# Transposed activations with four row tiles side by side, and weight slots that begin at multiples of 128 bytes

## The chip, the cores and the metric

The kernel runs on one core of a Trainium2 chip. The metric is the device time of one execution in microseconds; the time before is 1054.98 us, the median of 3 runs (1054.74 to 1055.16). Lower is better.

## What is computed

One layer of a hybrid decoder, for 1024 rows (positions) of 1024 features, all in float32:

```python
h = rms_norm(x, mix_norm)
z = h @ w_in                       # 1024 x 2320: gq, gk, gv, gr, glr, sq, sk, sv
o_gla = gla_chunked(gq, gk, gv, log_a)            # 4 heads, chunks of 64
o_gla = rms_norm(o_gla, gla_norm) * silu(gr)
o_swa = swa_sink_attention(sq, sk, sv, sinks)     # 8 heads, window 128
x = x + concat([o_gla, o_swa]) @ w_out
h2 = rms_norm(x, ffn_norm)
u = causal_dwconv(h2 @ w_up, conv_w, conv_b)      # 1024 x 5632, three taps
a, b = split(u, 2)
return x + (silu(a) * b) @ w_down                 # 2816 x 1024
```

## The kernel before

Every large product is made in float32r with each operand split into a high part and a low part (`split`, `tr_hi`, `tr_lo`: the high part is a copy rounded to float32r, the low part the difference). A product of two such operands is three passes of matmuls, `PASSES = ((0, 0), (0, 1), (1, 0))`, which sum in one PSUM bank. The 1024 rows are 8 row tiles `t` of 128, the 1024 features 8 tiles `k` of 128.

**The activations.** `big` holds the transposed activations of the stage that runs: features on the 128 partitions, and in each partition for each row tile `t`, feature tile `k` and part `r` (0 high, 1 low) 128 float32 values of the rows. It is filled three times: by the first norm (`norm1_tr`, `norm1_lo`), by the mixer's output (`gate_tr`), and by the second norm (`norm2_tr`, `norm2_sums`). A write covers four feature tiles `k` of one row tile and one part, that is four pieces of 128 values. `ex` holds three more such operands for the feed-forward part: sums and differences of quarters of the transposed activations, made in `norm2_sums`.

**The dense stages.** In `dense` (L317; the first three q tiles go through `unit_q_part`, L707) the weights that TensorE loads are 128 x 128 tiles of `big`, and the moving operand is a 128 x 512 tile of split weights. One row tile takes 8 feature tiles x 3 passes = 24 matmuls of 512 columns; for k and v of the window attention (tiles dk) the columns are 272. The names in the profile: dq, dk, dv, dg, dr for the parts of `w_in`, do for `w_out`.

**The feed-forward part.** `w_up` is taken in 22 chunks of 128 columns for a and 128 for b. Each chunk is a 2 x 2 block product by Strassen's scheme, seven products P1 to P7 (`product`, L834) of 4 feature tiles x 3 passes = 12 matmuls. Here the roles are turned round: the loaded weights are 128 x 128 tiles of the chunk's split operand (A11, A12, A22, S1 to S4), and the moving operand is 512 rows, four row tiles at once, of `big` (B11, B21, B22, T1) or `ex` (T2, T3, T4), given by `b_operand`. `w_down` goes by pairs of chunks with seven products too (`down_pair`, L1015, six matmuls at a time, both operands in slots): from chunk 2 on, one such piece of six follows each up product of twelve. The last two chunks go through `last_row` (L1044), where both operands are in slots and nothing comes from `big`.

**The order.** All work is entered in a list of events with times (`at`, `at_us`), which are sorted once, and a dependency-tracking layer places it on the engines' queues; no queue order depends on addresses.

**The places in the memory.** Nearly all split weights and the split gate live in nine slots of 4096 bytes a partition (`slot_tile`, pool `wa`: high part 2048 bytes, low part 2048 bytes), which lie at the upper end of the memory. The pool on the right side is filled from the upper end down. The memory that tiles can have ends at byte 229344 of a partition, which is 96 past a multiple of 128, so that before, with the slots uppermost, each slot begins 96 bytes past a multiple of 128 (192480, 196576, ...). `big` begins at 1152 and `ex` at 112448, both multiples of 64. The first two up operands of chunk 1 (`A11w_1`, `A12w_1`) are not in a slot but in the pool of the second norm, at multiples of 64; the weights of dk lie, but for the last feature tile, in a tile `kw` that begins at a multiple of 64 and has rows of 1088 bytes, a multiple of 64.

`mhalf` is a constant tile, -0.5, the exponent of the power that GpSimd takes in `rms_scale` and `norm1_stat`; it is at most 8 columns wide in use.

Of the kernel before, what the change touches and what calls it, by code (L numbers as in the profile page):

```python
# [9 lines left out]
F32 = mybir.dt.float32  # L10
F32R = mybir.dt.float32r
# [6 lines left out]
P = 128  # L18
T = 1024
D = 1024  # L20
NT = T // P
KD = D // P
# [12 lines left out]
def hymba_layer_kernel(ctx, tc, x, mix_norm, w_in, w_alpha2, b_alpha, gla_norm,  # L35
# [3 lines left out]
    act, dve, pool, pe, sp = nc.scalar, nc.vector, nc.gpsimd, nc.tensor, nc.sync  # L39
# [10 lines left out]
    base = ctx.enter_context(tc.tile_pool(name="base", bufs=1))  # L50
# [4 lines left out]
    def bank(name):  # L55
        ps["n"] += 1
        if "f" in ps:
            return ps["f"][2 + ps["n"] % 2]

        for start, which in (("n2pt_6", "b"), ("do1_7", "a"), ("n2pt_3", "a")):  # L60
            if name.startswith(start):
                return ps[which].tile([P, 512], F32, tag="b", name=name)
        return ps["ab"[ps["n"] % 2]].tile([P, 512], F32, tag="b", name=name)

    big = base.tile([P, NT, KD, 2, P], F32R, name="big")

    RAW_BUFS, K4, K2, N_WARM = 3, 6, 5, 5

    def raw_tile(name):
        return base.tile([P, 1024], F32, tag="raw", name=name, bufs=RAW_BUFS)  # L70

    w_keep = ctx.enter_context(tc.tile_pool(name="wa", bufs=1, side="right"))
    w_late = {}
    swp = ExitStack()
    idp = swp.enter_context(tc.tile_pool(name="idp", bufs=1, side="right"))
# [14 lines left out]
    def split(src, hi, lo, eng=None, hi_eng=None):  # L90
        if hi_eng is None:
            act.copy(hi, src)
        else:
            hi_eng.tensor_copy(hi, src)
        (eng or pool).tensor_sub(lo, src, hi.bitcast(F32))  # L95
# [19 lines left out]
    upper = gl.tile([P, P], F32, name="upper")  # L115
    amask = upper.bitcast(I32)
    ind = gl.tile([P, 2], F32R, name="ind")
    mhalf = idp.tile([P, 8], F32, name="mhalf")
    pool.memset(mhalf, -0.5)

    ones_r = gl.tile([P, P], F32R, name="ones_r")
# [67 lines left out]
    def norm1_lo(t, i):  # L189
        tr_lo(t, i, "n1")  # L190
# [32 lines left out]
    def norm2_sums(t):  # L223

        i, ex, pn = t - 4, fin["ex"], fin["pn"]
        p0, p1 = fin["pb", t]

        def put(src, dst):
            split(src, dst[:, :, 0, :], dst[:, :, 1, :], dve)

        b12 = pn.tile([P, 4, P], F32, tag="b12", name=f"b12_{t}", bufs=1)
        b11, b21 = big[:, i, 0:4].bitcast(F32), big[:, i, 4:8].bitcast(F32)
        act.copy(b12, p0)
        put(p1, big[:, t, 4:8])
        dve.tensor_sub(p0, p0, b11[:, :, 0, :])
        dve.tensor_sub(p0, p0, b11[:, :, 1, :])
        put(p0, big[:, t, 0:4])
        dve.tensor_sub(p1, p1, b12)
        put(p1, ex[:, 1, i])
        dve.tensor_add(p1, p1, b11[:, :, 0, :])  # L240
        dve.tensor_add(p1, p1, b11[:, :, 1, :])
        put(p1, ex[:, 0, i])
        dve.tensor_sub(p0, b21[:, :, 0, :], p1)
        dve.tensor_add(p0, p0, b21[:, :, 1, :])
        put(p0, ex[:, 2, i])

    trs = {}

    def tr_hi(t, q, h, tag):
        pt = bank(f"{tag}pt_{t}_{q}")  # L250
        for k in range(4):
            c = (q * 4 + k) * P
            pe.transpose(pt[:, k * P:(k + 1) * P], h[:, c:c + P], ident)
        trs[tag, t, q] = pt.rearrange("p (k c) -> p k c", k=4)
        act.copy(big[:, t, q * 4:q * 4 + 4, 0, :], trs[tag, t, q])

    def tr_lo(t, q, tag):
        hi, lo = big[:, t, q * 4:q * 4 + 4, 0, :], big[:, t, q * 4:q * 4 + 4, 1, :]
        dve.tensor_sub(lo, trs[tag, t, q], hi.bitcast(F32))

    def norm_tr(t, h, tag):
# [5 lines left out]
    blocks = {}  # L267
# [45 lines left out]
    def dense(t, ws, n, name):  # L313
        pb = bank(name)
        for k in range(KD):
            for i, (ra, rb) in enumerate(PASSES):
                pe.matmul(pb[:, :n], lhsT=big[:, t, k, ra, :], rhs=ws[k][:, rb, :n],  # L317
                          start=(k == 0 and i == 0), stop=(k == KD - 1 and i == 2))
        return pb

# [299 lines left out]
    def gate_tr(t, gs):  # L620
        pb = bank(f"ogt{t}")
        for h in range(4):
            pe.transpose(pb[:, h * P:(h + 1) * P], gs[:, h * P:(h + 1) * P], ident)
        pv = pb.rearrange("p (h c) -> p h c", h=4)
        hi, lo = big[:, t, 0:4, 0, :], big[:, t, 0:4, 1, :]
        act.activation(hi, pv, AF.Copy, scale=glan)
        dve.scalar_tensor_tensor(lo, pv, glan, hi.bitcast(F32), op0=ALU.mult, op1=ALU.subtract)
        src = qo[:, t, :].rearrange("p (j c) -> p j c", j=4)
        hi, lo = big[:, t, 4:8, 0, :], big[:, t, 4:8, 1, :]
        split(src, hi, lo)  # L630


    fin = {}
# [19 lines left out]
    def open_norm2():  # L653
        st.close()
        w_late["pool"] = swp.enter_context(tc.tile_pool(name="wb", bufs=1, side="right"))
        xp = ctx.enter_context(tc.tile_pool(name="xp", bufs=1))
        fin["ex"] = xp.tile([P, 3, 4, 4, 2, P], F32R, name="ex")
        fin["sn"] = ExitStack()
        pn = fin["pn"] = fin["sn"].enter_context(tc.tile_pool(name="pn", bufs=1))
        ffn = fin["ffn"] = pn.tile([P, D], F32, name="ffn")  # L660
        sp.dma_start(ffn, ffn_norm.partition_broadcast(P).rearrange("p o d -> p (o d)"))
        fin["s1"] = pn.tile([P, 4, P], F32, name="s1_0")
# [37 lines left out]
    def unit_q_part(t, k0, k1):  # L700
        if k0 == 0:
            psb["q", t] = bank(f"dq{t}")
        pb = psb["q", t]
        for k in range(k0, k1):

            for i, (ra, rb) in enumerate(((0, 0), (1, 0), (0, 1))):
                pe.matmul(pb, lhsT=big[:, t, k, ra, :], rhs=blocks["q"][k][:, rb, :],  # L707
                          start=(k == 0 and i == 0), stop=(k == KD - 1 and i == 2))

    def q_done(t):  # L710
# [2 lines left out]
    def unit_q(t):  # L713
        q_post(t, dense(t, blocks["q"], 512, f"dq{t}"))

    def unit_k(t):
        kvl_post(t, dense(t, blocks["k"], 272, f"dk{t}"))
# [81 lines left out]

    def b_operand(name, k, r):  # L800
        ex = fin["ex"]
        return {"B11": big[:, 0:4, k, r, :], "B21": big[:, 0:4, 4 + k, r, :],
                "B22": big[:, 4:8, 4 + k, r, :], "T1": big[:, 4:8, k, r, :],
                "T2": ex[:, 0, :, k, r, :], "T3": ex[:, 1, :, k, r, :],
                "T4": ex[:, 2, :, k, r, :]}[name]

    PROD = {"P1": ("A11", "B11"), "P2": ("A12", "B21"), "P3": ("S4", "B22"), "P4": ("A22", "T4"),
            "P5": ("S1", "T1"), "P6": ("S2", "T2"), "P7": ("S3", "T3")}
# [12 lines left out]
    def product(ch, name):  # L821
        an, bn = PROD[name]
        w = blocks["u", ch, an]
        onto = ONTO.get(name)
        if ch == 0 and name == "P3":
            onto = None
        if onto is None:
            psb[name, ch] = up_bank(ch, {"P1": 0, "P2": 1, "P3": 2, "P5": 2 if ch else 3}[name])
        pb = psb[name, ch] = psb[onto or name, ch]
        steps = [(k, ra, rb) for k in range(4) for ra, rb in PASSES]  # L830
        if ch == 0:
            steps.sort(key=lambda step: step[2])
        for i, (k, ra, rb) in enumerate(steps):
            pe.matmul(pb, lhsT=w[:, ra, k, :], rhs=b_operand(bn, k, rb),  # L834
                      start=(onto is None and i == 0), stop=(i == 11), skip_group_check=onto is not None)
# [253 lines left out]
    for c in halves:  # L1089
        split(mix_row[:, c], mix_hl[0][0:1, c], mix_hl[1][0:1, c], dve)  # L1090
        pb = bank(f"mix{len(mix_ps)}")
# [41 lines left out]
    for t in range(NT):  # L1133
        if t > 1:
            if t > 3:
                at(t - 2.7, load_x, t)
                at(t - 2.5, norm1, t)
                at(t - 1.6, lambda tt=t: norm_tr(tt, xts["h", tt], "n1"))
            if t > 2:
                at(TQ + t, unit_q, t)  # L1140
        at(TK + 0.6 * t, unit_k, t)
        at(TK + 0.6 * t + 1.9, kvl_tr, t)
        at(TK + 0.6 * t + 3.1, kvl_la, t)
        at(TV + t, unit_v, t)
        at(TG + t, unit_g, t)
        at(TR + t, unit_r, t)
        at(TO + t, unit_o, t, 0)
        u = TO + 8 + (2 * t if t < 4 else 2 * t - 7)
        at(u, unit_o, t, 1)
        at(u + 0.005, norm2_rows, t)  # L1150
        if t < 7:
            at(u + 1.9, norm2_tr, t)
        if 4 <= t < 7:
            at(u + SUMS, norm2_sums, t)
# [33 lines left out]
    at(TO + 8.006, mark)  # L1188
    at(TO - 0.05, open_acc)
    at(TO + 1.35, open_norm2)  # L1190
    def at_us(us, f, *a):
        at(TU + us / 5.2, f, *a)
# [18 lines left out]
    for ch, i, name in order:  # L1211
# [7 lines left out]
        if ch < 2 or (ch, i) == (2, 0):  # L1219
            n = 0  # L1220
        elif ch < L - 1 or (ch, i) == (L - 1, 0):
            n = 1
        else:
            n = 2
# [15 lines left out]
    at_us(-12, behind, first_sums)  # L1240
    at_us(0.28, norm2_tr, 7)
    at_us(0.29, norm2_sums, 7)
    at_us(1.76, load_side, 1, 1)
    for n, (ch, name, t0) in enumerate(prods):
# [4 lines left out]
    for p in range(NPAIR):  # L1249
        for k in range(7):  # L1250

            n = 7 * p + k - 2
# [51 lines left out]
```

## Time and profile before

| what | value |
|---|---|
| median of 3 runs | 1054.98 us |
| span of the profiled execution | 1053.6 us; the median of the runs is 1.4 us above it |
| TensorE busy | 1046.6 us, 4976 matmuls |
| weight loads (PEld) | 851.0 us, 4976 |
| VectorE / ScalarE / GpSimd busy | 799.4 / 480.2 / 617.7 us |
| DMA | 67.13 MB, mean 64 GB/s |

Engines: PE is TensorE's matmuls, PEld its weight loads, which run beside the matmuls, DVE is VectorE, ACT ScalarE, POOL GpSimd, SP SyncE. L834 is line 834 of the kernel before. Matmuls are pipelined: one starts before the one ahead has left the array, and the ends shown are modelled. A matmul's shown length (390 to 400 ns at 512 columns) is therefore no price; the price is the time from its start to the start of the next.

### The profile page before, as it was taken

Reading aid. Unit: us, or ns where it says so; the run is one execution under the profiler, and the core shown is the slowest. Engines: PE = TensorE matmul, PEld = TensorE weight load, DVE = VectorE, ACT = ScalarE, POOL = GpSimd, SP = SyncE. Lnnn points to the kernel's source line nnn. Section 1 sums busy time; section 2 is a strip of 40 time slices with the busy share of each in tenths; the row PEclk is TensorE's granted clock in tenths of the full one; section 3 lists DMA queues with packets and bytes.
Section 4 is the critical chain, followed back from the end, with each engine's and each line's share of the span. In section 5 each row is a group of like instructions: output and inputs, shape, how many; then the busy total and the mean of one; then the engine's idle time right before and its main releaser. Section 6 shows DMA issues by size and latency. Waiting matters only on the chain.

```text
span 1053.6 us, 13921 instructions
## 1 busy us (share of the span) xinstructions
PE 1046.6 (99%) x4976; PEld 851.0 (81%) x4976; DVE 799.4 (76%) x1332; ACT 480.2 (46%) x988; POOL 617.7 (59%) x510
## 2 busy tenths in 40 slices
PE   9999999999999999999999999999999999999998
PEld 6898877888888888888888888888888888888887
DVE  6776667754131699887979898897979798897976
ACT  5527655444340346554444445444444444444441
POOL 4592132325450205867868687877778687978750
PEclk9999999999999999999999999999999999999999
DMA  6152113002044202112121111212121211121104
GB/s 213 61 152 61 44 49 92 21 1 81 1 122 159 60 1 80 40 41 81 40 80 34 49 51 49 60 61 61 40 80 40 61 40 45 56 61 60 41 20 160
DMA packets 67502, 67.13 MB, mean 64 GB/s; under 512 B 4648, under 2 KB 52201, under 8 KB 67434
## 3 DMA queue, kind: packets, MB, share of 16 engines
q1 hardware_dynamic: 63448, 61.27, 18.7%
q10 hardware_dynamic: 3986, 4.99, 2.0%
q8 instruction: 39, 0.64, 0.2%
q14 instruction: 29, 0.24, 0.1%
HBM read 57.33 MB, written 4.19 MB: 58 GB/s over the span
## 4 chain that ended last, share of the span: by engine, by line
PE 97%; DMA 1%; DVE 1%; ACT 0%; issue 0%; POOL 0%; DVEq 0%; ACTq 0%; SPq 0%
PE fb L834 39%; PE dn_P L1015 18%; PE do L317 9%; PE dr L317 4%; PE dv L317 4%; PE dg L317 4%; PE dq L317 3%; PE dk L317 2%; PE gb L834 2%; PE dq L707 1%; PE pv L490 1%; PE dl L1044 1%; PE fb L1044 1%; PE go L600 1%; PE ga L591 1%; PE sc L443 1%
## 5 line engine op out<-in xcount | busy, mean ns | idle before, releaser
L1019 DVE TENSOR_TENSOR acc<-acc,dn_P 128x1024 f32<-128x1024 f32 x140 | 169.8, 1214 | 65.6 <-PE dn_P L1015 65.5
L1015 PE MATMUL dn_P<-dw,dg 128*128 128x512 f32 x840 | 215.8, 392 | 0.0
L1015 PEld LDWEIGHTS dn_P<-dw,dg 128*128 128x128 f32 x840 | 157.7, 188 | 37.1
L317 PE MATMUL do<-wow,big 128*128 128x512 f32 x384 | 92.9, 398 | 0.0
L317 PEld LDWEIGHTS do<-wow,big 128*128 128x128 f32 x384 | 71.1, 188 | 16.3
L95 POOL TENSOR_TENSOR dw<-dn,dw 128x512 fp32r<-128x512 f32 x50 | 69.1, 1381 | 25.3 <-PE dn_P L1015 19.5
L886 ACT COPY ca<-fb 128x512 f32<-128x512 f32 x62 | 36.3, 585 | 72.8 <-PE fb L834 72.7
L834 PE MATMUL fb<-big,A11w 128*128 128x512 f32 x252 | 63.0, 396 | 0.0
L834 PE MATMUL fb<-big,S4w 128*128 128x512 f32 x252 | 62.9, 396 | 0.0
L834 PE MATMUL fb<-big,S1w 128*128 128x512 f32 x252 | 62.9, 396 | 0.0
L834 PE MATMUL fb<-ex,S2w 128*128 128x512 f32 x252 | 62.8, 396 | 0.0
L834 PE MATMUL fb<-ex,S3w 128*128 128x512 f32 x252 | 62.8, 396 | 0.0
L841 DVE SCALAR_TENSOR_TENSOR ua<-fb,cc,ua 128x511 f32<-128x511 f32 x84 | 62.2, 740 | 0.5 <-ACT ua L846 0.3
L834 PE MATMUL fb<-big,A12w 128*128 128x512 f32 x252 | 62.5, 396 | 0.0
L834 PE MATMUL fb<-ex,A22w 128*128 128x512 f32 x252 | 62.5, 397 | 0.0
L834 PEld LDWEIGHTS fb<-big,A11w 128*128 128x128 f32 x252 | 47.4, 188 | 11.6
L834 PEld LDWEIGHTS fb<-big,S1w 128*128 128x128 f32 x252 | 47.4, 188 | 11.6
L834 PEld LDWEIGHTS fb<-big,S4w 128*128 128x128 f32 x252 | 47.4, 188 | 11.6
L834 PEld LDWEIGHTS fb<-ex,S2w 128*128 128x128 f32 x252 | 47.4, 188 | 11.4
L834 PEld LDWEIGHTS fb<-ex,A22w 128*128 128x128 f32 x252 | 47.4, 188 | 11.4
L834 PEld LDWEIGHTS fb<-ex,S3w 128*128 128x128 f32 x252 | 47.4, 188 | 11.4
L834 PEld LDWEIGHTS fb<-big,A12w 128*128 128x128 f32 x252 | 47.3, 188 | 11.1
(432 smaller groups left out, 2402.7 us busy)
## 6 DMA issues: line engine op xcount, KB each, us to landing
up<-in_w_up_dram SPq DMA_DIRECT2D x44, 512.0 KB, 3.9
dn<-in_w_down_dram SPq DMA_DIRECT2D x22, 512.0 KB, 3.5
acc<-in_x_dram SPq DMA_DIRECT2D x8, 512.0 KB, 6.9
out_dram<-acc SPq DMA_DIRECT2D x15, 256.0 KB, 2.0
xt<-in_x_dram SPq DMA_DIRECT2D x7, 512.0 KB, 3.4
vraw<-in_w_in_dram SPq DMA_DIRECT2D x4, 512.0 KB, 3.7
graw<-in_w_in_dram SPq DMA_DIRECT2D x4, 512.0 KB, 3.6
qt<-qt ACTq DMA_DIRECT2D x16, 128.0 KB, 2.2
```

The source lines that it names most:

```text
L95: (eng or pool).tensor_sub(lo, src, hi.bitcast(F32))
L317: pe.matmul(pb[:, :n], lhsT=big[:, t, k, ra, :], rhs=ws[k][:, rb, :n], start=(k == 0 and i == 0), stop=(k == KD - 1 and i == 2))
L443: pe.matmul(pbs[-1][:, j % 2, :], lhsT=ql[:, g, qc], rhs=kt[:, g, kc], start=False, stop=True)
L490: pe.matmul(pbs[i][HALF[g]], lhsT=vv[rows, t - 1 + b, HALF[g]], rhs=rhs[rows, :, HALF[i]], start=start, stop=stop)
L591: pe.matmul(pb[:, pr * 256:(pr + 1) * 256], lhsT=gqt[t][:, pr, :], rhs=qbd[t % 2][:, pr], start=(pr == 0), stop=(pr == 1))
L600: pe.matmul(pb[:, h * P:(h + 1) * P], lhsT=asb[:, h, :], rhs=v[:, h * P:(h + 1) * P], start=(h == 0), stop=(t == 0 and h == 3))
L834: pe.matmul(pb, lhsT=w[:, ra, k, :], rhs=b_operand(bn, k, rb), start=(onto is None and i == 0), stop=(i == 11), skip_group_check=onto is n ...
L841: dve.scalar_tensor_tensor(dst, src, w, dst, op0=ALU.mult, op1=ALU.add)
L886: act.copy(dst, pb)
L1015: pe.matmul(pb[:, i], lhsT=g[:, ra, c:c + P], rhs=w[:, rb, :], start=(onto is None and n == 0), stop=(n == 2), skip_group_check=onto is no ...
L1019: dve.tensor_add(acc, acc, pb)
L1044: pe.matmul(pb[:, c0:c1], lhsT=g[:, ra, (t % 4) * P:(t % 4 + 1) * P], rhs=w[:, rb, c0:c1], start=(ch == NCH - 2 and i == 0), stop=(ch == N ...
```

## The change

Three things change in the code.

- `big` goes from `[row tile, feature tile, part, 128]` to `[half, feature tile, part, row tile in the half, 128]`, and `ex` likewise. Four row tiles of one feature tile and part are then 512 consecutive values (2048 bytes), where they were four pieces of 512 bytes, 8192 bytes apart in `big` and 4096 in `ex`. What is read as weights, 128 values, is one piece before and after. A write of four feature tiles of one row tile has four pieces of 512 bytes before and after; they lie 1024 bytes apart before and 4096 after.
- `mhalf` is made 24 columns wide (96 bytes) and is put in a pool of its own, `edge`, opened before the slots' pool on the right side. It takes the 96 bytes at the upper end, and each slot begins at a multiple of 128 (192384, 196480, ...).
- `mhalf` leaves the pool `idp`, 32 bytes. What lies below the slots on that side (`ident`, `qo`, `vg`, `kw`, the x tiles) begins 64 bytes lower than before; all of it stays at multiples of 64. `big` and `ex` begin where they did.

On all five engines the built program has the same instructions in the same order with the same waits; only the memset of `mhalf` is wider (128x24 for 128x8).

```diff
-    big = base.tile([P, NT, KD, 2, P], F32R, name="big")
+    big = base.tile([P, 2, KD, 2, 4, P], F32R, name="big")
+
+    def rows(t, ks, r):
+        return big[:, t // 4, ks, r, t % 4, :]
...
+    edge = ctx.enter_context(tc.tile_pool(name="edge", bufs=1, side="right"))
+    mhalf = edge.tile([P, 24], F32, name="mhalf")
     w_keep = ctx.enter_context(tc.tile_pool(name="wa", bufs=1, side="right"))
...
-    mhalf = idp.tile([P, 8], F32, name="mhalf")
     pool.memset(mhalf, -0.5)
...
-        act.copy(big[:, t, q * 4:q * 4 + 4, 0, :], trs[tag, t, q])
+        act.copy(rows(t, slice(q * 4, q * 4 + 4), 0), trs[tag, t, q])
...
-                pe.matmul(pb[:, :n], lhsT=big[:, t, k, ra, :], rhs=ws[k][:, rb, :n],
+                pe.matmul(pb[:, :n], lhsT=rows(t, k, ra), rhs=ws[k][:, rb, :n],
...
-        fin["ex"] = xp.tile([P, 3, 4, 4, 2, P], F32R, name="ex")
+        fin["ex"] = xp.tile([P, 3, 4, 2, 4, P], F32R, name="ex")
...
-        return {"B11": big[:, 0:4, k, r, :], "B21": big[:, 0:4, 4 + k, r, :],
-                "B22": big[:, 4:8, 4 + k, r, :], "T1": big[:, 4:8, k, r, :],
-                "T2": ex[:, 0, :, k, r, :], "T3": ex[:, 1, :, k, r, :],
-                "T4": ex[:, 2, :, k, r, :]}[name]
+        return {"B11": big[:, 0, k, r], "B21": big[:, 0, 4 + k, r],
+                "B22": big[:, 1, 4 + k, r], "T1": big[:, 1, k, r],
+                "T2": ex[:, 0, k, r], "T3": ex[:, 1, k, r], "T4": ex[:, 2, k, r]}[name]
```

`tr_lo`, `gate_tr`, `unit_q_part` and `norm2_sums` get the same indexing by `rows`, and nothing else.

More of the change, by code (lines that the diff above doesn't have):

```diff
@@ L226, in norm2_sums, with put, extra, own @@
         p0, p1 = fin["pb", t]
-        def put(src, dst):
-            split(src, dst[:, :, 0, :], dst[:, :, 1, :], dve)
+        def put(src, hi, lo):
+            split(src, hi, lo, dve)
+        def extra(n):
+            return ex[:, n, :, 0, i, :], ex[:, n, :, 1, i, :]
+        def own(ks):
+            return rows(t, ks, 0), rows(t, ks, 1)
         b12 = pn.tile([P, 4, P], F32, tag="b12", name=f"b12_{t}", bufs=1)
-        b11, b21 = big[:, i, 0:4].bitcast(F32), big[:, i, 4:8].bitcast(F32)
+        b11, b21 = ([rows(i, ks, r).bitcast(F32) for r in range(2)] for ks in (slice(0, 4), slice(4, 8)))
         act.copy(b12, p0)
[L234 to L237, printed above, removed]
+        put(p1, *own(slice(4, 8)))
+        dve.tensor_sub(p0, p0, b11[0])
+        dve.tensor_sub(p0, p0, b11[1])
+        put(p0, *own(slice(0, 4)))
         dve.tensor_sub(p1, p1, b12)
[L239 to L245, printed above, removed]
+        put(p1, *extra(1))
+        dve.tensor_add(p1, p1, b11[0])
+        dve.tensor_add(p1, p1, b11[1])
+        put(p1, *extra(0))
+        dve.tensor_sub(p0, b21[0], p1)
+        dve.tensor_add(p0, p0, b21[1])
+        put(p0, *extra(2))
     trs = {}
@@ L254, in tr_hi @@
         trs[tag, t, q] = pt.rearrange("p (k c) -> p k c", k=4)
-        act.copy(big[:, t, q * 4:q * 4 + 4, 0, :], trs[tag, t, q])
+        act.copy(rows(t, slice(q * 4, q * 4 + 4), 0), trs[tag, t, q])
     def tr_lo(t, q, tag):
-        hi, lo = big[:, t, q * 4:q * 4 + 4, 0, :], big[:, t, q * 4:q * 4 + 4, 1, :]
+        hi, lo = (rows(t, slice(q * 4, q * 4 + 4), r) for r in range(2))
         dve.tensor_sub(lo, trs[tag, t, q], hi.bitcast(F32))
@@ L624, in gate_tr @@
         pv = pb.rearrange("p (h c) -> p h c", h=4)
-        hi, lo = big[:, t, 0:4, 0, :], big[:, t, 0:4, 1, :]
+        hi, lo = (rows(t, slice(0, 4), r) for r in range(2))
         act.activation(hi, pv, AF.Copy, scale=glan)
@@ L628, in gate_tr @@
         src = qo[:, t, :].rearrange("p (j c) -> p j c", j=4)
-        hi, lo = big[:, t, 4:8, 0, :], big[:, t, 4:8, 1, :]
+        hi, lo = (rows(t, slice(4, 8), r) for r in range(2))
         split(src, hi, lo)
@@ L706, in unit_q_part @@
             for i, (ra, rb) in enumerate(((0, 0), (1, 0), (0, 1))):
-                pe.matmul(pb, lhsT=big[:, t, k, ra, :], rhs=blocks["q"][k][:, rb, :],
+                pe.matmul(pb, lhsT=rows(t, k, ra), rhs=blocks["q"][k][:, rb, :],
                           start=(k == 0 and i == 0), stop=(k == KD - 1 and i == 2))
```

## The prediction

> **What bounds the kernel now.** I read the page first, then what TensorE waits for, then the timeline of TensorE in one stage after another, and last the merged chain.
>
> ```profile
> span 1053.6 us, 13921 instructions
> ...
> PE 1046.6 (99%) x4976; PEld 851.0 (81%) x4976; DVE 799.4 (76%) x1332; ACT 480.2 (46%) x988; POOL 617.7 (59%) x510
> ...
> PEclk9999999999999999999999999999999999999999
> ...
> PE 97%; DMA 1%; DVE 1%; ACT 0%; issue 0%; POOL 0%; DVEq 0%; ACTq 0%; SPq 0%
> ```
>
> The chain that ended last is TensorE for 97% of the span, at full granted clock. The page's 99% alone would prove little, since ends of matmuls are modelled; the waits say it better. These are all the waits of TensorE that the trace can name:
>
> ```profile
> PE warm L1085 <- DVE warm L124: 1.7, 1, 1.7
> PE dg L317 <- ACT vg L720: 0.9, 1, 0.9
> PE dq L707 <- POOL qw L295: 0.3, 1, 0.3
> PE gb L834 <- ACT big L255: 0.2, 1, 0.2
> PE dq L707 <- DVE big L259: 0.2, 1, 0.2
> ```
>
> They come to 3.3 us. So time can come from the distance between one matmul and the next. Since that distance isn't a column anywhere, I take it as the difference of two starts in the timeline, divided by the count. Two turns of the feed-forward loop (columns: start, length with a modelled end, engine, line, tiles, count):
>
> ```profile
> 615.77 2.97 PE L834 MATMUL fb<-big,A11w 128*128 128x512 f32 x12
> 618.58 1.54 PE L1015 MATMUL dn_P<-dw,dg 128*128 128x512 f32 x6
> 619.96 2.97 PE L834 MATMUL fb<-big,A12w 128*128 128x512 f32 x12
> 622.76 1.54 PE L1015 MATMUL dn_P<-dw,dg 128*128 128x512 f32 x6
> 624.14 2.98 PE L834 MATMUL fb<-ex,S2w 128*128 128x512 f32 x12
> ```
>
> Twelve up matmuls (L834) last 618.58 - 615.77 = 2.81 us, 234 ns each; six down matmuls (L1015) last 1.38 us, 230 ns each. From the chain (start, time on the chain, what), the other dense stages:
>
> ```profile
> 77.93 3.04 PE dk L317 x24
> 81.63 3.00 PE dk L317 x24
> ...
> 228.26 5.60 PE dg L317 x24
> ...
> 312.97 47.83 PE do L317 x205
> ...
> 1033.74 2.72 PE dl L1044 x12
> 1036.46 2.72 PE fb L1044 x12
> ```
>
> The dense projections (dg, do: L317) take 5.60/24 = 47.83/205 = 233.3 ns, the last rows (L1044) only 2.72/12 = 226.7 ns, all with 512 columns; dk with 272 columns takes 125 to 127. The same shape and type thus costs 226.7, 230, 233.3 or 234 ns, and nobody waits. What differs is where the two operands begin in their partition. I write it as the remainder by 64 bytes, moving operand first, weights second: last rows 32/32; down 32/32; projections 32/0 (weights are `big`); up 0/32, the moving operand in four pieces of 512 bytes; dk 0/0 for seven of its eight weight tiles. Equal remainders go with the fast rows, unequal ones with the slow rows.
>
> Is it the place, or something else that differs between those lines? One short stretch changes the place alone:
>
> ```profile
> 404.85 1.10 PE L834 MATMUL gb<-big,A11w 128*128 128x512 f32 x4
> 405.79 2.46 PE L834 MATMUL fb<-big,A11w 128*128 128x512 f32 x10
> 408.09 1.09 PE L834 MATMUL gb<-big,A12w 128*128 128x512 f32 x4
> 409.02 0.39 PE L834 MATMUL fb<-big,A11w 128*128 128x512 f32 x1
> ```
>
> The gb rows use weights of chunk 0 in slots (remainder 32), the ten fb matmuls weights of chunk 1, whose first two tiles are not in a slot and begin at a remainder of 0. The moving operand is the same part of `big`. The intervals: 0.94/4 = 235 ns, 2.30/10 = 230, 0.93/4 = 233. And the down products are slower than the last rows although both are 32/32, because they follow up products:
>
> ```profile
> 1027.36 2.97 PE L834 MATMUL fb<-big,S4w 128*128 128x512 f32 x12
> 1030.16 0.86 PE L1044 MATMUL fb<-dnw,g 128*128 128x512 f32 x3
> 1030.86 1.52 PE L1044 MATMUL dl<-dnw,g 128*128 128x512 f32 x6
> 1032.21 1.52 PE L1044 MATMUL fb<-dnw,g 128*128 128x512 f32 x6
> ```
>
> After twelve up matmuls the first three fast-placed ones still take 0.70/3 = 233 ns; the next six 1.35/6 = 225, on the way to 226.7. Whatever is lost recovers only after some matmuls, so a slow product taxes the six down matmuls behind it.
>
> **The change, part by part.** The built program has the same instructions in the same order with the same waits on all five engines; one memset is wider and addresses and steps differ. So nothing is added or moved in any queue, and the sum is made of intervals.
>
> *Slots at multiples of 128, and four row tiles side by side.* Afterwards all of these products are 0/0, and the up products read one piece of 2048 bytes. The 0/0 case with one piece of 512 columns isn't in the trace. Nearest rows: 226.7 ns (L1044, equal remainders, one piece, 512 columns, a long run) and dk, 0/0 in a long run, 125.8 on average. Between these two long runs the 240 columns of difference cost (226.7 - 125.8)/240 = 0.42 ns each, which says that a matmul carries the same fixed part at 0/0 as at 32/32. The cheap end comes from the scores, 0/0 with 256 columns, in bursts of eight of which six starts are even:
>
> ```profile
> 175.81 0.28 PE L442 MATMUL sc<-kt,qt 128*128 128x256 f32 x1
> ...
> 176.38 0.28 PE L443 MATMUL sc<-kt,ql 128*128 128x256 f32 x1
> ```
>
> Five intervals in 0.57 us, 114 ns; with 256 more columns at 0.42 that is 221.5. The dear end is the 230 of the ten matmuls above. I take 226.7: it is a long run of this very shape, as the products here are, and the scores are a short burst.
>
> - Up: 22 chunks x 7 products x 12 = 1848 matmuls, 234.2 to 226.7: 13.9 us.
> - Projections q (from row tile 3), v, g, r, o: 1080 matmuls of 512 columns, 233.3 to 226.7: 7.1 us. The 72 matmuls of the first three q tiles I leave out, as they lie in the start, where data are late; dk has 0/0 already.
> - Down: 840, 230 to 226.7, since no slow product stands ahead any more: 2.8 us.
>
> Together 23.8 us, all on TensorE, which sets the end. The ten fb matmuls above ran faster by 3 to 5 ns for the place of their weights alone. The Trainium skill (TensorE: Matmul & The Clock Gate, Step-by-step: what each phase is for) says that TensorE has two independent read ports, so that loading the next tile's weights takes no bandwidth from the running matmul; by that rule the place of weights is worth nothing, and at 4 ns for 1848 matmuls the sum would be smaller by 7.4 us. The row disagrees with the rule.
>
> *Who must keep up.*
>
> ```profile
> 460.00:975.00 515.00, 515.00 (x2212) 415.45 (x2211) 449.19 (x557) 238.90 (x404) 398.33 (x292) 1.00 0.18 55
> DVE acc L1019 <- PE dn_P L1015: 65.5, 61, 3.1
> ```
>
> From 460 to 975 us VectorE (third pair) is busy for 449 of 515 us, and it is VectorE that waits for down products, 65.5 us in 61 waits. A loop turn of 4.08 us in place of 4.19 leaves 515 x 0.973 = 501 us for these 449; the cover holds until the turn is 13% shorter. Before 460 us some waits have little room, the first up product behind the casts of its weights above all; I take 1 us of the gain back for them.
>
> *Writes into `big` and `ex` with steps of 4096 bytes in place of 1024 between the four pieces.*
>
> ```profile
> 409.22 0.62 ACT L92 CAST A22w<-up 128x512 fp32r<-128x512 f32 x1 [1.63 <-PE gb L834]
> 410.70 0.60 ACT L92 CAST big<-fb 128x512 fp32r<-128x512 f32 x1
> 411.17 0.61 ACT L92 CAST ex<-n2pt 128x512 fp32r<-128x512 f32 x1
> ```
>
> One piece (A22w) costs as much as four, so I take 0. No row has the wider step; at 0.1 us more or less for each of the some 15 such operations of a row tile in the second norm it is 1.5 us a tile on engines that TensorE mostly doesn't wait for. *The constant* of 24 columns: before, its memset of 8 took 0.10 us on GpSimd, off the chain; 0.
>
> Sum: 23.8 - 1 = 22.8 us, which makes the span 1030.8. The median of the runs, 1054.98, lies 1.4 above the span: 1032.2, say 1032.
>
> **The rivals.**
>
> *Half of it.* Only the weights' place counts, and only where the moving operand is streamed from `big` or `ex`: up 234.2 to 230, 7.8 us, nothing elsewhere: 1047; with some of the effect of one piece down to 1037. For it: the projections read weights from `big` at remainder 0 already and are slow. Against it: then the last rows, with weights at 32, should be the slowest.
>
> *More than that.* Every such matmul comes down to 221.5: 1848 x 12.7 + 840 x 8.5 + 1080 x 11.8 = 43.3 us, 1013 after the same 1 us. For it the scores; against it dk. The Trainium skill (same page, Wait — 56 ns, not 53.3 ns?) gives 215.7 ns for back-to-back matmuls of 512 columns; by that the time would be, as an estimate, some 989 us, and no row here shows an interval that short.
>
> *No change.* What I read as place goes with the product (which tile is weights, the order of its passes): 1055. Against it: ten matmuls between two groups of four, with the line, order and moving operand unchanged. The Trainium skill (SBUF — State Buffer, Specifications) knows lines of 16 bytes only; all old places are multiples of 16, so by it nothing changes. The 226.7 against 233.3 speaks against it.
>
> *Slower.* Operands that begin at the same place of a 128-byte stretch collide when weights load beside the stream. Priced by the difference seen between pairings, 6.6 ns, with the sign turned: 3768 x 6.6 = 25 us, 1080. It decides as soon as the mean interval rises by 0.6 ns. Against it: 32/32, the same place too, is the fastest row.
>
> **How the numbers follow.** Full gain 0.58, half 0.17, more 0.14, no change 0.06, slower 0.05. 0.2% (2.1 us) is about what this measurement can tell from no change. Faster is 0.58 + 0.17 + 0.14 = 0.89. The range goes from the end of the cheap case, 1012, to most of the half case, 1046; it leaves out no change, slower, the upper part of the half case and what might lie below 221.5, some 0.2. The forecast's own range is 1024 to 1037.
>
> **What the changed profile should show.** A dg or dr row of 24 in 5.44 us and not 5.60; up products of 12 in 2.72 and a loop turn of 4.08; down products of six in 1.36, level from the first; dk still 3.0 and the last rows still 2.72; the same 1.00 clock; VectorE's wait for dn_P shorter, TensorE's waits up by a microsecond or so. Up at 229 to 230 with the projections at 233 means the half case. Up below 224 means that 32/32 was itself not free. The forecast is wrong in kind if L1044 or dk move too, as remainders then weren't the cause, or if the rows fall but TensorE gets waits for VectorE or GpSimd.

## The result

The changed kernel takes 1039.14 us (median of 4 runs, 1038.54 to 1039.35), the kernel before 1054.86 us on the same chip: a ratio of 0.9851, 95% interval 0.9837 to 0.9865. It is faster by 15.7 us, where 23 were forecast. The time lies in the prediction's range of 1012 to 1046, but outside the 1024 to 1037 that it called the forecast's own.

The page of the profile after, in the lines that answer to those shown of before:

```profile
span 1037.4 us, 13921 instructions
...
PE 1030.0 (99%) x4976; PEld 849.3 (82%) x4976; DVE 793.4 (76%) x1332; ACT 480.6 (46%) x988; POOL 618.4 (60%) x510
...
PEclk9999999999999999999999999999999999999999
...
PE 97%; DMA 1%; DVE 1%; ACT 0%; issue 0%; POOL 0%; DVEq 0%; ACTq 0%; SPq 0%
```

The same instructions, the same clock, the same chain: TensorE sets the end as before, and its busy time fell by 16.6 us. The waits of TensorE are those of before to a few tenths; the two longest:

```profile
PE warm L1094 <- DVE warm L128: 1.7, 1, 1.7
PE dg L327 <- ACT vg L730: 1.0, 1, 1.0
```

So the time came from the distance between matmuls. The chain (start, time on the chain, what) for dk, dg, do and the last rows; `dense` is now L327, the up product L843, down L1024, the last rows L1053:

```profile
76.30 3.00 PE dk L327 x24
...
189.29 5.46 PE dg L327 x24
...
308.60 46.51 PE do L327 x205
...
1017.48 2.72 PE dl L1053 x12
1020.20 2.72 PE fb L1053 x12
```

The long run of do has come from 233.3 to 46.51/205 = 226.9 ns a matmul, dg from 5.60 to 5.46 a row tile; dk and the last rows stand where they stood. But in the feed-forward loop (timeline of TensorE) only the turns whose product reads `big` got what was forecast:

```profile
610.52 2.88 PE L843 MATMUL fb<-big,A12w 128*128 128x512 f32 x12
613.24 1.52 PE L1024 MATMUL dn_P<-dw,dg 128*128 128x512 f32 x6
614.60 2.96 PE L843 MATMUL fb<-ex,S2w 128*128 128x512 f32 x12
617.40 1.54 PE L1024 MATMUL dn_P<-dw,dg 128*128 128x512 f32 x6
618.78 2.88 PE L843 MATMUL fb<-big,S1w 128*128 128x512 f32 x12
```

A product that reads `big` takes 613.24 - 610.52 = 2.72 us (226.7 ns a matmul) and the down piece behind it 1.36 (226.7). A product that reads `ex` still takes 617.40 - 614.60 = 2.80 us (233.3), and the down piece behind it 1.38. Three of the seven products read `ex`: 792 of the 1848 up matmuls, 5.2 us at 6.6 ns each, and about 1 us in the down pieces behind them. That is some 6 of the missing 7 us, and the first thing to explain: what is wrong with `ex`, which by the remainder by 64 bytes lies as well as `big`.

The table shows how each kernel's places and its mean intervals go together; the sections behind it say what each kernel is. The means are worked out from all rows of a trace: the distance from the start of each 512-column matmul to the next start on TensorE, leaving out distances over 270 ns, which hold a wait or other work. "Apart" is the beginning of the moving operand less that of the weights, modulo 256 bytes (the remainder that is left by 256), in the built program.

| kernel | projections: apart, ns | up from `big`: apart, ns | up from `ex`: apart, ns | down (0 apart), ns | median, us |
|---|---|---|---|---|---|
| before | 96, 233.3 | 160, 234.0 | 96, 234.4 | 230.4 | 1054.98 |
| after | 0, 228.3 | 0, 227.0 | 192, 233.3 | 228.0 | 1039.14 |
| layout_alone | 96, 233.3 | 160, 234.0 | 96, 234.4 | 230.4 | 1054.67 |
| slots_alone | 0, 228.3 | 0, 227.0 | 192, 233.3 | 228.0 | 1039.08 |
| ex_at_128 | 0, 228.3 | 0, 226.8 | 0, 226.8 | 226.7 | 1033.05 |
| slots_at_64 | 64, 229.5 | 192, 233.2 | 128, 232.6 | 229.7 | 1048.05 |
| equal_at_192 | 64, 229.6 | 192, 233.4 | 0, 226.8 | 228.6 | 1042.52 |
| cc_above | 128, 232.6 | 128, 232.6 | 128, 232.7 | 229.3 | 1049.57 |
| slots_at_160 | 32, 233.1 | 224, 233.4 | 160, 233.9 | 229.8 | 1053.11 |

The projections at 0 apart keep a mean of 228.3, since a row tile's first matmuls behind other work are slower; in the long run of do they are at 226.9.

### The profile page after: what moved, and what is told of

Its sections match the earlier page's. It is cut to its first block, busy times and chain, and to the rows that moved or that the text cites. A ratio compares the mean times of both kernels' runs of the same rounds, so it can differ in the third digit from the quotient of the medians.

```text
span 1037.4 us, 13921 instructions
## 1 busy us (share of the span) xinstructions
PE 1030.0 (99%) x4976; PEld 849.3 (82%) x4976; DVE 793.4 (76%) x1332; ACT 480.6 (46%) x988; POOL 618.4 (60%) x510
## 4 chain that ended last, share of the span: by engine, by line
PE 97%; DMA 1%; DVE 1%; ACT 0%; issue 0%; POOL 0%; DVEq 0%; ACTq 0%; SPq 0%
PE fb L843 39%; PE dn_P L1024 18%; PE do L327 8%; PE dr L327 4%; PE dg L327 4%; PE dv L327 4%; PE dq L327 3%; PE dk L327 2%; PE gb L843 2%; PE dq L717 1%; PE pv L500 1%; PE fb L1053 1%; PE dl L1053 1%; PE go L610 1%; PE ga L601 1%; PE sc L453 1%
## 5 line engine op out<-in xcount | busy, mean ns | idle before, releaser
L1028 DVE TENSOR_TENSOR acc<-acc,dn_P 128x1024 f32<-128x1024 f32 x140 | 169.9, 1215 | 61.5 <-PE dn_P L1024 60.3
L1024 PE MATMUL dn_P<-dw,dg 128*128 128x512 f32 x840 | 214.0, 390 | 0.0
L1024 PEld LDWEIGHTS dn_P<-dw,dg 128*128 128x128 f32 x840 | 157.6, 188 | 34.5
L327 PE MATMUL do<-wow,big 128*128 128x512 f32 x384 | 90.9, 393 | 0.0
L327 PEld LDWEIGHTS do<-wow,big 128*128 128x128 f32 x384 | 71.1, 188 | 14.4
L843 PE MATMUL fb<-ex,S2w 128*128 128x512 f32 x252 | 62.5, 394 | 0.0
L843 PE MATMUL fb<-ex,S3w 128*128 128x512 f32 x252 | 62.5, 394 | 0.0
L843 PE MATMUL fb<-ex,A22w 128*128 128x512 f32 x252 | 62.2, 394 | 0.0
L843 PE MATMUL fb<-big,A11w 128*128 128x512 f32 x252 | 61.2, 389 | 0.0
L843 PE MATMUL fb<-big,S1w 128*128 128x512 f32 x252 | 61.1, 389 | 0.0
L843 PE MATMUL fb<-big,S4w 128*128 128x512 f32 x252 | 61.1, 389 | 0.0
L843 PE MATMUL fb<-big,A12w 128*128 128x512 f32 x252 | 60.9, 390 | 0.0
L843 PEld LDWEIGHTS fb<-ex,S2w 128*128 128x128 f32 x252 | 47.2, 187 | 11.3
L843 PEld LDWEIGHTS fb<-ex,A22w 128*128 128x128 f32 x252 | 47.2, 187 | 11.3
L843 PEld LDWEIGHTS fb<-ex,S3w 128*128 128x128 f32 x252 | 47.2, 187 | 11.3
L843 PEld LDWEIGHTS fb<-big,S1w 128*128 128x128 f32 x252 | 47.3, 188 | 10.0
L843 PEld LDWEIGHTS fb<-big,A11w 128*128 128x128 f32 x252 | 47.3, 188 | 10.0
L843 PEld LDWEIGHTS fb<-big,S4w 128*128 128x128 f32 x252 | 47.3, 188 | 10.0
L843 PEld LDWEIGHTS fb<-big,A12w 128*128 128x128 f32 x252 | 47.2, 188 | 9.8
```

The costliest lines, as they stand in the source:

```text
L327: pe.matmul(pb[:, :n], lhsT=rows(t, k, ra), rhs=ws[k][:, rb, :n], start=(k == 0 and i == 0), stop=(k == KD - 1 and i == 2))
L1024: pe.matmul(pb[:, i], lhsT=g[:, ra, c:c + P], rhs=w[:, rb, :], start=(onto is None and n == 0), stop=(n == 2), skip_group_check=onto is no ...
L1028: dve.tensor_add(acc, acc, pb)
```

## The experiments

Each ratio is to the kernel before, run beside it: a median of 1054.70 us for the first four kernels, 1054.84 for the next three.

**`ex` moved by 64 bytes.** `ex` began at 112448, which is 64 past a multiple of 128. A tile of 64 bytes (`expad`) goes ahead of it. To make room, `mhalf` gets 8 columns again, and two small tiles `e` of the feed-forward pool move up beside it, so that the slots stay where they are.

```diff
-    mhalf = edge.tile([P, 24], F32, name="mhalf")
+    mhalf = edge.tile([P, 8], F32, name="mhalf")
...
+        xp.tile([P, 16], F32, name="expad")
         fin["ex"] = xp.tile([P, 3, 4, 2, 4, P], F32R, name="ex")
...
-        e = psb[key, ch] = fin["ff"].tile([P, 2], F32, tag="e", name=f"{key}_{ch}", bufs=2)
+        e = psb[key, ch] = edge.tile([P, 2], F32, tag="e", name=f"{key}_{ch}", bufs=2)
```

> The changed kernel with ex begun 64 bytes later, at a multiple of 128 (the two 8-byte edge tiles move out of the feed-forward pool to make room). Theory of equal remainders by 128 (a matmul of one piece of 512 columns starts 226.7 ns after the one ahead when moving operand and weights begin at the same remainder by 128 bytes, else 233.3): the 792 up matmuls from ex go from 233.3 to 226.7, 5.2 us, and the down matmuls that follow them lose their slow first three, 1 us: 1033 us. Rival, that ex itself is slow (its place in the memory or who writes it): rows from ex stay at 2.80 us for twelve, 1039 us.

Measured: 1033.05 us (1032.62 to 1033.29), ratio 0.9792 [0.9777, 0.9807]. Its timeline:

```profile
612.29 2.88 PE L844 MATMUL fb<-ex,S2w 128*128 128x512 f32 x12
615.01 1.52 PE L1025 MATMUL dn_P<-dw,dg 128*128 128x512 f32 x6
616.37 2.88 PE L844 MATMUL fb<-big,S1w 128*128 128x512 f32 x12
619.09 1.52 PE L1025 MATMUL dn_P<-dw,dg 128*128 128x512 f32 x6
```

Products from `ex` and from `big` now take the same 2.72 us and every down piece 1.36: the turn of 4.08 us that was forecast. So the place of `ex` cost 6.1 us, and not who writes it. This is also the best version of the study.

**The two parts of the change by themselves.** One kernel has the new layout, with `mhalf` back in `idp` and the slots where they were:

```diff
-    edge = ctx.enter_context(tc.tile_pool(name="edge", bufs=1, side="right"))
-    mhalf = edge.tile([P, 24], F32, name="mhalf")
...
+    mhalf = idp.tile([P, 8], F32, name="mhalf")
```

> The new layout of big and ex alone; the slots stay at a remainder of 96. Equal remainders: up matmuls are 0/96 and 64/96 in one piece, 233.3 ns and not 226.7, against 234.2 in four pieces before: 1848 x 0.9 = 1.7 us, 1053 us, projections at 233.3 as before. Rival, that the one piece is what made the up products fast: twelve from big in 2.72 us, 1046 us or less.

Measured: 1054.67 us, ratio 1.0001 [0.9992, 1.0011], and each mean interval of the table as before. The long run of do in its chain, 233.3 ns a matmul as in the kernel before:

```profile
311.75 47.83 PE do L326 x205
```

The other has the kernel before, with the moving operand in four pieces, and only the 96 bytes above the slots:

```diff
+    edge = ctx.enter_context(tc.tile_pool(name="edge", bufs=1, side="right"))
+    mhalf = edge.tile([P, 24], F32, name="mhalf")
     w_keep = ctx.enter_context(tc.tile_pool(name="wa", bufs=1, side="right"))
...
-    mhalf = idp.tile([P, 8], F32, name="mhalf")
```

> The slots at multiples of 128 alone; big and ex keep the old layout, four pieces. Equal remainders: projections 226.7 (24 in 5.44 us), down level at 226.7 behind big, up from big at 0/0 226.7 plus some 0.9 for the four pieces, up from ex (64/0) 229 to 234: 1039 to 1042 us. Rival, that the one piece is needed: up rows of twelve stay at 2.80 or 2.81, only the projections and some of down gain: 1046 us or more.

Measured: 1039.08 us, ratio 0.985 [0.9835, 0.9865]: the whole change. In its timeline a moving operand in four pieces of 512 bytes is as quick as one of 2048 where the places agree, and as slow where they don't:

```profile
611.01 2.88 PE L835 MATMUL fb<-big,A12w 128*128 128x512 f32 x12
613.73 1.52 PE L1016 MATMUL dn_P<-dw,dg 128*128 128x512 f32 x6
615.09 2.96 PE L835 MATMUL fb<-ex,S2w 128*128 128x512 f32 x12
617.89 1.54 PE L1016 MATMUL dn_P<-dw,dg 128*128 128x512 f32 x6
```

2.72 us from `big`, 2.80 from `ex`. The four row tiles side by side are worth nothing; the constant of 24 columns above the slots brings the whole gain.

**Slots at 64 past a multiple of 128.** One line of the changed kernel; it asks whether equal remainders by 128 bytes are enough, also when they are 64 and not 0.

```diff
-    mhalf = edge.tile([P, 24], F32, name="mhalf")
+    mhalf = edge.tile([P, 8], F32, name="mhalf")
```

> The changed kernel with a constant of 8 columns, so that the slots begin at a remainder of 64 by 128. Equal remainders: up from ex (64/64) becomes fast, 2.72 us for twelve, up from big (0/64) and the projections (64/0) slow, 2.80 for twelve and 5.60 for 24, down fast: 1039.1 + 7.0 + 7.0 - 5.2 = 1048 us. Rival, that a true multiple of 128 is what counts: everything is slow, 1054 us. Rival of remainders by 64, which the prediction used: everything is fast, 1032 us.

Measured: 1048.05 us, ratio 0.9936 [0.992, 0.9953]. The total agreed with the forecast of 1048, the rows did not:

```profile
613.87 2.96 PE L843 MATMUL fb<-big,A12w 128*128 128x512 f32 x12
616.67 1.54 PE L1024 MATMUL dn_P<-dw,dg 128*128 128x512 f32 x6
618.05 2.95 PE L843 MATMUL fb<-ex,S2w 128*128 128x512 f32 x12
620.84 1.54 PE L1024 MATMUL dn_P<-dw,dg 128*128 128x512 f32 x6
```

Products from `ex`, which by 128 now lies at 64 as the slots do, should have taken 2.72 and took 2.79; the projections, which should have been as slow as before, had a mean of 229.5 ns. Two misses of opposite sign made a right sum. So remainders by 128 were the wrong measure as well. By 256, `ex` (64) and the slots (192) lie 128 apart there. What fits all rows so far is: quickest where both operands begin at the same remainder by 256. The next three kernels were chosen to break that.

**All places at multiples of 128, but 128 apart by 256.** The convolution's coefficients, 704 bytes, go above the slots.

```diff
-    mhalf = edge.tile([P, 24], F32, name="mhalf")
+    mhalf = edge.tile([P, 8], F32, name="mhalf")
+    cc = edge.tile([P, 4, 44], F32, name="cc")
...
-    cc = base.tile([P, 4, 44], F32, name="cc")
```

> The new layout with the conv coefficients (tile cc, 704 bytes) and a 32-byte mhalf above the slots, so that all places are multiples of 128 bytes, but by 256 the slots begin at 0 (191744), big at 128 (1152) and ex at 128 (111744). Theory now: a 512-column matmul is at its quickest, 226.7 ns, only where moving operand and weights begin at the same remainder by 256 bytes. Then up (moving 128, weights 0) and the projections (moving 0, weights 128) are slow, 233 ns each, and only down and the last rows are level; the whole 1053 us (1049 to 1055), although every place is a multiple of 128. Rival, remainder by 128 (or multiples of 128) is what counts: all products at 226.7, 1033 us. Rival, ex was slow for where it lies among the other tiles and not for its remainder: projections and big at 226.7, ex at 233: 1039.

Measured: 1049.57 us, ratio 0.9954 [0.9937, 0.9972]. The timeline:

```profile
616.66 2.95 PE L843 MATMUL fb<-big,A12w 128*128 128x512 f32 x12
619.45 1.54 PE L1024 MATMUL dn_P<-dw,dg 128*128 128x512 f32 x6
620.82 2.96 PE L843 MATMUL fb<-ex,S2w 128*128 128x512 f32 x12
623.62 1.54 PE L1024 MATMUL dn_P<-dw,dg 128*128 128x512 f32 x6
```

and the chain:

```profile
311.15 47.64 PE do L328 x205
```

Up products take 2.79 and 2.80 us, do 47.64/205 = 232.4 ns. Beginning at a multiple of 128 helps nothing if the two operands are 128 apart; with 128 as the period it would have been 1033. The loss is slightly smaller than before (232.6 for 233.3 to 234.4), which makes up most of the 5 us.

**Equal, and at no multiple of 128.** Slots at 192 by 256 as in slots_at_64, and `ex` moved to 192 too: the 64 bytes of `expad`, and as many because the tiles `e` now lie in the pool ahead of `ex`.

```diff
-    mhalf = edge.tile([P, 24], F32, name="mhalf")
+    mhalf = edge.tile([P, 8], F32, name="mhalf")
...
+        xp.tile([P, 16], F32, name="expad")
         fin["ex"] = xp.tile([P, 3, 4, 2, 4, P], F32R, name="ex")
...
-        e = psb[key, ch] = fin["ff"].tile([P, 2], F32, tag="e", name=f"{key}_{ch}", bufs=2)
+        e = psb[key, ch] = base.tile([P, 2], F32, tag="e", name=f"{key}_{ch}", bufs=2)
```

> Slots at 64 past a multiple of 128 again (192448, 192 by 256), as in the run that gave 1048.05, but ex is moved to the same remainder (112576, 192 by 256); big stays at 128. Theory, equal remainders by 256: the three up products that read ex come down from 233 to 226.7 ns, those from big stay at 233 and the projections at 229; 792 x 6.3 = 5.0 us and about 1 us for the down products behind them: 1042 (1040 to 1044). Rival, only multiples of 128 are quick, equal or not: ex stays at 233, 1048. Rival, ex at 128 by 256 was itself what made it quick: 1048 as well.

Measured: 1042.52 us, ratio 0.9887 [0.9871, 0.9903].

```profile
613.44 2.96 PE L844 MATMUL fb<-big,A12w 128*128 128x512 f32 x12
616.24 1.54 PE L1025 MATMUL dn_P<-dw,dg 128*128 128x512 f32 x6
617.62 2.88 PE L844 MATMUL fb<-ex,S2w 128*128 128x512 f32 x12
620.34 1.52 PE L1025 MATMUL dn_P<-dw,dg 128*128 128x512 f32 x6
```

The picture of the changed kernel turned round: `ex` at 2.72 and `big` at 2.80. Where an operand lies doesn't decide; what counts is that the two lie alike. Nor is the measure longer than 256 bytes: by 512, `big` (1152) and the slots (192384) lie 256 apart in the changed kernel, and its up products from `big` are at 227.0 all the same.

**Two differences not yet seen.** `mhalf` of 16 columns, slots at 160 by 256.

```diff
-    mhalf = edge.tile([P, 24], F32, name="mhalf")
+    mhalf = edge.tile([P, 16], F32, name="mhalf")
```

> The new layout with 64 bytes above the slots: slots at 160 by 256, so that the differences moving - weights by 256 are 224 (up from big), 160 (up from ex), 32 (projections), 0 (down, last rows): two differences not yet seen. Theory, the cost rises by degrees with the difference (0: 226.7 ns, 64: 229, 96 to 192: 233 to 234): projections at 227 to 229, up from big between 226.7 and 233, say 230, up from ex at 234: about 1045 (1039 to 1050). Rival, any difference but 0 costs the whole 6.6 ns: 1054, as before, with projections at 233 too. Rival, the lines are 64 bytes and a difference under 64 costs nothing on either side: projections and big at 226.7, ex at 234: 1039.

Measured: 1053.11 us, ratio 0.9985 [0.9976, 0.9995]. The expectation that the cost rises by degrees failed: 32 bytes apart cost as much as 96. `mhalf` has left `idp` here too, so that this part of the change isn't what brought the gain.

The long run of do in its chain, and a turn of the loop in its timeline:

```profile
311.44 47.83 PE do L327 x205
```

```profile
618.00 2.96 PE L843 MATMUL fb<-big,A12w 128*128 128x512 f32 x12
620.80 1.55 PE L1024 MATMUL dn_P<-dw,dg 128*128 128x512 f32 x6
```

do takes 233.3 ns at 32 apart, up 2.80 us at 224 apart. Every difference but 0 costs some 6 ns, with one exception: 64 (moving operand 64 above the weights) costs about a quarter of that in the projections of both kernels that have it (229.5 and 229.6 against 228.3 and 233.3), while 192, the same distance the other way, costs all of it. Even 64 isn't always cheap. The ten fb matmuls on `A11w` that the prediction shows, at 230 ns, are 64 apart; in slots_at_64 their own places are the same, and its timeline has

```profile
400.57 2.50 PE L843 MATMUL fb<-big,A11w 128*128 128x512 f32 x10
402.91 1.08 PE L843 MATMUL gb<-big,A12w 128*128 128x512 f32 x4
```

2.34/10 = 234 ns. What stands ahead of them may count too; no run settles it.

**The same, with half the columns.** dk, with 272 columns and rows of 1088 bytes so that its places go through four remainders, took about 126 ns on average in every kernel. Either short matmuls don't have the loss, or alternation hides it. Each 512-column projection is made as two of 256:

```diff
-                pe.matmul(pb[:, :n], lhsT=rows(t, k, ra), rhs=ws[k][:, rb, :n],
-                          start=(k == 0 and i == 0), stop=(k == KD - 1 and i == 2))
+                for c in ([slice(0, 256), slice(256, 512)] if n == 512 else [slice(0, n)]):
+                    pe.matmul(pb[:, c], lhsT=rows(t, k, ra), rhs=ws[k][:, rb, c],
+                              start=(k == 0 and i == 0 and c.start == 0), stop=(k == KD - 1 and i == 2 and c.stop == n))
```

once in ex_at_128 (0 apart, run halves_equal) and once in layout_alone (96 apart, run halves_apart).

> The version with every product equal by 256 bytes (slots and big and ex at 128), in which each projection matmul of 512 columns is made as two of 256 with the same weights: 48 of them for a row tile instead of 24. Base of a comparison: if a matmul at equal places costs its columns and the same fixed part as at 512 (226.7 - 512/2.4 = 13.3 ns), 120 ns each, 5.76 us for a row tile, and 45 row tiles make the whole 14 us longer: 1047 us. If the scores' 114 ns (256 columns) are the price: 5.47 us and 1034.

> The same halving of the projections in the version with the new layout and the slots where they were before (moving operand at 224, weights at 128 by 256). At 512 columns unequal places cost 6.6 ns a matmul more. If the loss is paid once a matmul (with its weight load): 6.6 more than the run with halves at equal places, 126.7 ns, 6.08 us for a row tile, 1076 us. If it is paid by the column: 3.3 more, 123.3 ns, 5.92, 1069. If matmuls this short do not have it, as the tiles dk with 272 columns and mixed places suggest (125 to 126 ns in every version): 120 ns, 5.76, 1062.

One run each, so without an interval: 1045.88 and 1062.61 us. The chain of the first, and then of the second:

```profile
90.99 5.76 PE dv L328 x48
98.13 5.75 PE dv L328 x48
```

```profile
91.84 5.75 PE dv L327 x48
99.00 5.75 PE dv L327 x48
```

5.75/48 = 119.8 ns in both. At 256 columns the place costs nothing in the sum. It still shows in the single starts: in the long run of do they are 119 to 121 ns apart in the first kernel, and 113 to 125 in turn in the second, with a mean of 120 in both. So at 256 columns the place is felt, and it evens out. The two runs stay 16.7 us apart because their up products, still of 512 columns, and the down pieces behind them differ.

## Why the prediction was right, and where it was off

**What bounds the kernel** was read rightly: the gain is on TensorE alone, with no new wait above 0.3 us. VectorE's cover held, too:

```profile
DVE acc L1028 <- PE dn_P L1024: 60.3, 58, 3.0
```

It waits for down products 60.3 us in place of 65.5, and of the 1 us that the prediction took off for new waits of TensorE less than half was lost: its named waits rose from 3.3 to 3.7 us.

**The terms, with their sizes.** The mean intervals of before and after, times their counts:

- Up: 13.9 us forecast, 8.3 came: 7.4 from the 1056 matmuls that read `big`, and only 0.9 from the 792 that read `ex`. This is the step that failed: "Afterwards all of these products are 0/0". By 64 bytes they are. By 256, which the runs show to be the measure, `big` and the slots both lie at 128, but `ex` lies at 64, that is 192 apart, and stays at 233.3 ns.
- Projections: 7.1 forecast, 5.4 came. The level, 226.7, was right in the long run; the first matmuls of a row tile behind other work stayed slower, so that dg takes 5.46 to 5.49 and not 5.44.
- Down: 2.8 forecast, 2.0 came; the pieces behind a slow product still pay, as the prediction's own mechanism says.

Together 15.7 us, and the span of the profiled execution fell by 16.2.

**Right mechanism, wrong measure, and some luck.** That equal places are the quick ones was right. That multiples of 128 made the slots lie like `big` was luck: in cc_above all places are multiples of 128 as well, but the operands of the projections and of the up products lie 128 apart by 256, and the time was 1049.57 us.

**The row that could have told.** The ten fb matmuls on `A11w` in the trace of before, 230 ns between groups at 235 and 233, were read as 0/0 and put in as the dear end of the range. By 256 bytes they are 64 apart, the one difference that can cost only a part; with equal places by 256, in cc_above, the same matmuls have a median of 227. A middle value between two levels was a sign that the remainder was taken by too small a number. The prediction didn't follow it.

**dk** gave the right fixed part for a wrong reason: its places are mixed by 256 bytes, and it is quick most likely because matmuls this short don't pay, as the halves show at 256 columns. The fixed part holds: halves at equal places take 119.8 ns, and 226.7 less 256 columns at the prediction's 0.42 ns gives 119.2.

**The grouped part.** One piece for four was put into the same 7.5 ns as the slots' place; alone it is worth nothing (1.0001). Writes with the wider step and the wider memset cost nothing that shows, as forecast.

**The rivals.** Half: it has the projections stay at 233 and up products come down to 230; the projections fell to 228.3 and the up products from `big` to 227.0. That the total came between its 1047 and the forecast has another reason, the place of `ex`. More: 221.5 appears in no long run; the scores' 114 ns for 256 columns was a matter of a short burst, as the halves in a long run take 119.8. The Trainium skill (TensorE: Matmul & The Clock Gate, Wait — 56 ns, not 53.3 ns?) gives 215.7 ns back to back; no run here shows it, 226.7 is the lowest level of any long run. No change: by the lines of 16 bytes of the Trainium skill (SBUF — State Buffer, Specifications) nothing should have moved. All places here are multiples of 32, and the whole went from 1033.05 to 1054.67 by them. Slower: equal places are the quickest in each kernel.

The two independent read ports of the Trainium skill (TensorE: Matmul & The Clock Gate, Step-by-step: what each phase is for) fit the sum of the halves, where 96 bytes between the operands cost nothing, and not the 512-column products: slots_alone moves the weights alone, and its up matmuls from `big` go from 234.0 to 227.0 ns.

**Open** stays why. Every matmul loads its weights, so the runs can't say whether the load, the stream or both pay; nor why 64 one way costs a quarter and the other way all, nor where between 272 and 512 columns the loss begins. In the halves the same weights serve two matmuls in succession, which may matter; dk is made in the order of the 512-column projections, without halves, and is quick as well, which speaks against it.

## What to carry to other kernels

Where TensorE sets the end with long rows of 512-column float32r matmuls, look at the intervals between starts by product: if the same shape has two levels and nobody waits, compare where moving operand and weights begin modulo 256 bytes, and shift one tile so that they agree; here 96 bytes above the slots and 64 ahead of `ex` gave 2%. Test such a rule with a kernel that keeps the round number and breaks the equality, and one that does the reverse: a total that agrees (1048 for 1048) proved nothing until its rows did. Of a change with two parts run each alone; the one that had nearly all of the edited lines was worth nothing.

## What was not expected of the hardware

- 512-column float32r matmuls cost 226.7 ns each in a long row where both operands begin at the same remainder by 256 bytes, and 232 to 234.4 where they are 32, 96, 128, 160, 192 or 224 apart; at 64 mostly 229 to 230, and once, in ten matmuls, 234.
- At 256 columns it is 119.8 ns at 0 and at 96 apart; the single starts are even (119 to 121 ns) at 0 and uneven (113 to 125 ns) at 96.
- A moving operand in four pieces 8192 bytes apart is as quick as one of 2048 bytes (227.0 ns both, 1039.08 and 1039.14 us).
